# Memory attention placed in a recurrence's chunk loop, rope and weight sums beside seven-product pairs, and three more such pairs

## The chip, the cores and the metric

The kernel runs on one core of a Trainium2 chip. Its time is the device time of one execution in microseconds (us). Engines are named as the profile names them: PE multiplies matrices (PEld loads its weights), DVE, ACT and POOL work on vectors, SP issues most of the transfers (DMA). Each engine works through its own queue in order, and engines wait for one another by semaphores.

## The reference

One decoder layer on 1024 tokens of width 1024, in float32: a SwiGLU half-step (hidden width 2816), a mixer, another SwiGLU half-step, each with a norm ahead and behind. The mixer takes one projection `u @ w_in` and splits it for three branches, RWKV-7, windowed attention and cross-attention into 256 memory tokens, and 3 x 1024 gate columns:

```python
p_rwkv, p_swa, q_mem, gate_logits = _split(u @ w_in, IN_SIZES)
y_a = rwkv7_mix(p_rwkv, ...)                       # a recurrence over the tokens, 8 heads of 64
q_s, k_s = partial_rope(q_s, cos, sin), partial_rope(k_s, cos, sin)   # first 16 of 64 channels
y_b = sliding_window_gqa_sinks(q_s, k_s, v_s, swa_sinks)             # 8 query, 2 key heads, window 128
km, vm = jnp.split(mem_n @ w_kv, 2, axis=-1)
s = jnp.einsum('bshd,bmhd->bhsm', q_mem * 128 ** -0.5, km)           # 4 heads of 128
y_c = jnp.einsum('bhsm,bmhd->bshd', jax.nn.softmax(s, axis=-1), vm)
g_a, g_b, g_c = _split(jax.nn.sigmoid(gate_logits + gate_b), (D, D, D))
merged = g_a * (y_a @ w_branch[0]) + g_b * (y_b @ w_branch[1]) + g_c * (y_c @ w_branch[2])
h = h + rms_norm(merged @ w_out, mix_post_g)
```

## The kernel before

**Products.** A float32 product is made of three matmuls on values split in two: w_hi (ACT casts), w_lo (DVE subtracts), and the same for the moving side; L379 to L381 are the three. A strip is 128 output columns for 1024 tokens. A *plain* strip takes 8 blocks of the contraction x 2 halves of the tokens x 3 = 48 matmuls of 128x512. A *pair* of strips (`win_pair`) is done with seven products of 12 matmuls each (84 for two strips, 96 plainly), from sums of weights and of tokens: products collect in the PSUM tiles px, py and pz, ACT copies some to SBUF, and DVE adds them up (att<-px,part and so on) and so empties the banks.

**The order of the middle part.** First the pairs of `WIN_PAIRS`, nine of them, with gates 2 to 13 among them; beside pairs 4 to 7 a generator gives out small pieces of RWKV's triangular inverse between the products (`CORNER`). Then the RWKV chunk loop (`rwkv_chain`): 16 chunks of 64 tokens, each a chain of small matmuls (z, y, z, y, gram, z, and the transposes bkt) with DVE and ACT copies between. These take their PSUM banks in turn from one set of four (tag bg), so bkt waits until ACT has copied sv and uv out of y's bank. Behind each chunk's bkt stand six matmuls of gates 14 and 15, plain strips. POOL makes the weight sums (`ws`, L691) of three of the second SwiGLU's units beside the chunks, from loads issued on SP.

Then `rwkv_finish` (norm over the heads, and the output gate g_up: tiles ysq, var, yrs, gup), and `attention`: eight memory blocks of 128 tokens, then eight window blocks. A block has scores, soft (exponentials, shares), turn (transposes) and values. Between them PE is given *fill*: plain gate strips 16 to 23 and the branches' products, counted out by `FINISH` and `LUMPS`. The rope tables, k's rotation and each block's rotation of q run on DVE there, with the swapped channels loaded by small transfers. A branch's output goes to memory as y_d, and a scheduler places what is not kept in program order.

**Names.** msc: memory scores; mp, mst: exponentials, their maxima and sums; mptr, mpt: transposed shares in PSUM and SBUF; mpv, yo: values and output; km, vm, qm, kd: keys, values and queries.

Of the kernel before, what the change touches and what calls it, by code (L numbers as in the profile page):

```python
# [11 lines left out]
F32 = mybir.dt.float32  # L12
# [27 lines left out]
MAIN_PSUM = ("po", "px", "py", "pr", "pgate", "pq", "pb", "pw")  # L40
OPS = 8
KEEP = KP - OPS
LOOP_UNITS = 3
# [142 lines left out]
class MemoryBlock(Block):  # L186
    def soft(self, behind):
        pass

# [5 lines left out]
    def scores(self):  # L195
        V, S = self.nc.vector, self.nc.scalar
        scale = float(128 ** -0.5)
        banks = []
        st = self.pool.tile([P, 3, 4], F32, tag="mst", name="mst", bufs=2)
        for a in (0, 1):  # L200
# [3 lines left out]
            V.tensor_reduce(st[:, 0, 2 * a : 2 * a + 2], ps.rearrange("p (j k) -> p j k", k=MEM), AXX, ALU.max)  # L204
            banks.append(ps)
        V.tensor_scalar(st[:, 1], st[:, 0], -scale, None, ALU.mult)
        self.pr = self.pool.tile([P, 4, MEM], F32, tag="sc", name="mp", bufs=2)
        for i in range(4):
            S.activation(self.pr[:, i], banks[i // 2][:, (i % 2) * MEM : (i % 2 + 1) * MEM], ACT.Exp, scale=scale,
                         bias=st[:, 1, i : i + 1], accum_out=st[:, 2, i : i + 1])  # L210
        V.reciprocal(st[:, 0], st[:, 2])
        for i in range(4):
            V.tensor_scalar(self.pr[:, i], self.pr[:, i], st[:, 0, i : i + 1], 0.5, ALU.mult, ALU.mult)
        return last

    def turn(self):
        self.pt = self.pool.tile([P, 4, 2, P], F32, tag="pt", name="mpt", bufs=2)
        for a in (0, 1):
            ps = self.k.psum("mptr")
# [3 lines left out]
            self.copied = [self.nc.scalar.copy(self.pt[:, 2 * a : 2 * a + 2], ps.rearrange("p (j k c) -> p j k c", j=2, k=2))]  # L223
        return last

    def values(self):
        ps = self.k.psum("mpv")
        for h in range(4):
            for kt in (0, 1):
                self.mm(ps[:, h * P : (h + 1) * P], self.vm[:, kt, h * P : (h + 1) * P], self.pt[:, h, kt, :], start=kt == 0, stop=kt == 1)  # L230
        self.k.y_out(ps, self.y_d, self.b, self.pool)


class Builder:
# [364 lines left out]
    def ffn_in(self, f, x, form_d, first_d, parts, norm):  # L599

        nc, V = self.nc, self.nc.vector
        with self.tc.tile_pool(reuse_waits="tile", name="ffn_in", bufs=2) as pool:
# [13 lines left out]
            for j in range(KF):  # L616
                *pair, made = self.ffn_in_pair(f, j, pool, first_d)
                pairs.append(pair)
                skip = LOOP_UNITS if f == "ffn2" else 0
# [60 lines left out]
    def sums_in_loop(self, pool):  # L680

        beside, behind = {}, {}
        G = self.nc.gpsimd.tensor_tensor
# [1418 lines left out]
```

## Time and profile before

| what | number |
|---|---|
| median of 3 runs | 2245.7 us (2245.69 to 2249.21) |
| profiled execution, its span | 2246.46 us, 2244.6 us |
| PE, DVE, ACT, POOL busy | 2220.6, 1646.5, 1037.3, 96.7 us |
| chunk loop | about 1097 to 1204 us of the span |
| finish | about 1204 to 1234 us |
| memory blocks | 1234 to 1312 us |

A row of a timeline has start, length, engine, line, operation, output<-inputs, shape and count, and in brackets the idle time before it with what ended it. A row of windows has the stretch, its length, and for PE, PEld, DVE, ACT and POOL the busy time and the count; then the granted clock of PE as a share of full speed, the DMA share and GB/s. A row of waits has who waited for whom: total us, times, longest. Matmuls overlap, so the time of one is read from start to start.

### The profile page before, as it was taken

How to read it: one execution, taken by the hardware profiler on the slowest of the kernel's cores; microseconds unless marked ns; L12 is line 12 of the kernel's file. 1: busy time of each engine (PE TensorE's matmuls, PEld its weight loads, DVE VectorE, ACT ScalarE, POOL GpSimd, SP SyncE). 2: the span in 40 equal slices, each digit the busy share in tenths (PEclk: the TensorE clock that was granted, in tenths of full speed). 3: DMA queues.
4: the chain of work that ended last, by engine and by line, in shares of the span. 5: the costliest groups of instructions: out<-in, count | busy, mean ns of one | idle time of the engine just before them, and what ended most of it. 6: DMA issues, size and time to landing. Idle time of an engine off the chain costs nothing.

```text
span 2244.6 us, 34591 instructions
## 1 busy us (share of the span) xinstructions
PE 2220.6 (99%) x12280; PEld 1825.1 (81%) x12280; DVE 1646.5 (73%) x2769; ACT 1037.3 (46%) x1947; POOL 96.7 (4%) x166
## 2 busy tenths in 40 slices
PE   8999999999999999999999999999999999999998
PEld 6888888888887788888887887788888888887887
DVE  6988767766698887874467567794898887776576
ACT  6622333454555653444445564444663233345451
POOL 0000000000000011000253000000000000000000
PEclk9999999999999999999999999999999999999999
DMA  8565566686665446455574654464565555678663
GB/s 289 172 203 172 194 212 211 229 298 206 194 218 186 133 141 196 159 181 156 158 239 143 197 164 143 146 230 146 182 198 187 192 190 189 218 255 255 204 195 124
DMA packets 272236, 432.41 MB, mean 193 GB/s; under 512 B 50848, under 2 KB 89760, under 8 KB 271808
## 3 DMA queue, kind: packets, MB, share of 16 engines
q1 hardware_dynamic: 255392, 400.00, 55.1%
q10 hardware_dynamic: 15392, 29.17, 3.8%
q8 instruction: 96, 1.57, 0.3%
q0 software_dynamic: 1280, 1.05, 0.2%
q14 instruction: 76, 0.62, 0.1%
HBM read 292.75 MB, written 136.31 MB: 191 GB/s over the span
## 4 chain that ended last, share of the span: by engine, by line
PE 92%; DVE 4%; DMA 2%; issue 1%; ACT 1%; SPq 0%; DVEq 0%; ACTq 0%
PE px L379 9%; PE px L381 9%; PE px L380 9%; PE po L380 6%; PE po L381 6%; PE po L379 6%; PE pz L379 4%; PE pz L381 4%; PE pz L380 4%; PE pb L379 2%; PE pb L380 2%; PE pb L381 2%; PE pgate L379 2%; PE pgate L380 2%; PE pgate L381 2%; PE pr L379 2%
## 5 line engine op out<-in xcount | busy, mean ns | idle before, releaser
L302 ACT CAST w_hi<-w_raw 128x512 fp32r<-128x512 f32 x612 | 378.8, 620 | 696.9 <-PE px L380 191.7
L304 DVE TENSOR_TENSOR w_lo<-w_raw,w_hi 128x512 fp32r<-128x512 f32 x612 | 419.3, 687 | 182.3 <-ACT w_hi L302 164.7
L379 PE MATMUL po<-u,w_hi 128*128 128x512 f32 (+1 forms) x476 | 180.9, 380 | 0.0
L380 PE MATMUL po<-u,w_hi 128*128 128x512 f32 (+1 forms) x476 | 180.9, 380 | 0.0
L381 PE MATMUL po<-u,w_lo 128*128 128x512 f32 (+1 forms) x476 | 180.9, 380 | 0.0
L379 PE MATMUL px<-u,w_hi 128*128 128x512 f32 x388 | 151.2, 390 | 0.8 <-DVE km L1626 0.8
L379 PE MATMUL pz<-u,w_hi 128*128 128x512 f32 x388 | 151.2, 390 | 0.0
L381 PE MATMUL px<-u,w_lo 128*128 128x512 f32 x388 | 151.1, 389 | 0.0
L380 PE MATMUL px<-u,w_hi 128*128 128x512 f32 x388 | 150.9, 389 | 0.0
L380 PE MATMUL pz<-u,w_hi 128*128 128x512 f32 x388 | 150.9, 389 | 0.0
L381 PE MATMUL pz<-u,w_lo 128*128 128x512 f32 x388 | 150.9, 389 | 0.0
L379 PE MATMUL px<-f,w_hi 128*128 128x512 f32 x352 | 137.1, 390 | 0.3 <-DVE u L743 0.2
L380 PE MATMUL px<-f,w_hi 128*128 128x512 f32 x352 | 137.0, 389 | 0.0
L381 PE MATMUL px<-f,w_lo 128*128 128x512 f32 x352 | 136.9, 389 | 0.0
L488 DVE TENSOR_TENSOR u<-hid,u 128x512 fp32r<-128x512 f32 x114 | 78.4, 689 | 47.2 <-ACT u L487 46.5
L380 PEld LDWEIGHTS po<-u,w_hi 128*128 128x128 f32 x476 | 89.5, 188 | 17.2
L379 PEld LDWEIGHTS po<-u,w_hi 128*128 128x128 f32 x476 | 89.5, 188 | 17.0
L381 PEld LDWEIGHTS po<-u,w_lo 128*128 128x128 f32 x476 | 89.5, 188 | 16.8
L487 ACT CAST u<-hid 128x512 fp32r<-128x512 f32 x114 | 70.6, 620 | 66.0 <-DMA hid<-form_d 56.2
L379 PE MATMUL pr<-u,w_hi 128*128 128x512 f32 x224 | 87.6, 392 | 0.0
L380 PE MATMUL pr<-u,w_hi 128*128 128x512 f32 x224 | 87.3, 391 | 0.1
L381 PE MATMUL pr<-u,w_lo 128*128 128x512 f32 x224 | 87.2, 390 | 0.0
(451 smaller groups left out, 5213.9 us busy)
## 6 DMA issues: line engine op xcount, KB each, us to landing
w_raw<-in_ffn_in SPq DMA_DIRECT2D x224, 256.0 KB
hid<-form_d SPq DMA_DIRECT2D x154, 256.0 KB
w_raw<-in_win SPq DMA_DIRECT2D x112, 256.0 KB
form_d<-g SPq DMA_DIRECT2D x88, 256.0 KB
ws<-in_ffn_out SPq DMA_DIRECT2D x88, 256.0 KB
ffn_sum_d<-ws SPq DMA_DIRECT2D x88, 256.0 KB
w_raw<-ffn_sum_d SPq DMA_DIRECT2D x88, 256.0 KB
form_d<-h SPq DMA_DIRECT2D x66, 256.0 KB
```

Source lines behind the costliest of these rows:

```text
L302: self.nc.scalar.copy(hi, x)
L304: self.split_last = self.nc.vector.tensor_tensor(lo, x, hi.bitcast(F32), ALU.subtract)
L379: mm(out, wh, xh, start=first, stop=False, **kw)
L380: mm(out, wh, xl, start=False, stop=False, **kw)
L381: self.last_mm = mm(out, wl, xh, start=False, stop=last, **kw)
L487: self.nc.scalar.copy(hi, x)
L488: self.nc.vector.tensor_tensor(lo, x, hi.bitcast(F32), ALU.subtract)
```

## The change

1. **Three more pairs.** `GATES_FIRST` goes from 14 to 20: gates 14 to 19, plain before (two in the loop, four in the fill), become three pairs, twelve in all. `filling` starts with gate 21; gate 20 stays plain, most of it behind chunk 0.
2. **Memory attention in the loop.** Block i has its scores behind the odd chunk c = 2i + 1; the maxima and the exponentials in chunk c + 1, the shares there and in c + 2, the transposes behind chunk c + 2 and the values behind c + 3, with y_d stored from ACT's queue (`beside_chunks`). msc, mptr and mpv take banks of the other set of four (tag mm). The last blocks' remaining steps go into the finish (`between`). Gate 20's tanh and the table load for logarithm and exponential stand in chunk 1. `attention` has window blocks only, and the branches' order is 2, 0, 1.
3. **Rope and sums beside pairs 6 to 10.** `beside_pairs` gives out, between products: three units of weight sums (now on DVE), the rope tables, the rotation of k on DVE and of q on POOL in halves of 512 tokens, with loads on SP and stores to att_d on POOL. The inverse's pieces take pairs 4 and 5. Window blocks load rotated q and k.

The first place is PE's queue in the loop. Before, around one chunk's end:

```order
L1230 MATMUL y<-f,sv 64x64 x8
L1230 MATMUL z<-z,dinv 64x64 x8
L1230 MATMUL y<-center,f 64x64 x8
L1230 MATMUL gram<-f 128x128 x8
L1230 MATMUL z<-uv,bk 64x64 x8
L1270 MATMUL bkt<-ident,f 128x128 x4
L380 MATMUL pgate<-u,w_hi 128x512
L381 MATMUL pgate<-u,w_lo 128x512
L379 MATMUL pgate<-u,w_hi 128x512
```

Now, from an odd chunk's end to the next even chunk's:

```order
L1297 MATMUL bkt<-ident,f 128x128 x4
L105 MATMUL mptr<-ident,mp 128x128 x8
L102 MATMUL msc<-km_in,qm 128x256 x4
L1257 MATMUL z<-sv,gz 64x64 x8
L1257 MATMUL y<-gz,uv 64x64 x8
L1257 MATMUL y<-f,sv 64x64 x8
L1257 MATMUL z<-z,dinv 64x64 x8
L1257 MATMUL y<-center,f 64x64 x8
L1257 MATMUL gram<-f 128x128 x8
L1257 MATMUL z<-uv,bk 64x64 x8
L1297 MATMUL bkt<-ident,f 128x128 x4
L102 MATMUL mpv<-mpt,vm_in 128x128 x8
```

In the place of six gate matmuls stand a block's transposes and the next block's scores behind an odd chunk, and a block's values behind an even one.

The second place is ACT's queue in the same chunks. Before, one chunk and the end of the one ahead:

```order
L1250 COPY sv<-y 64x256 x2
L1250 COPY uv<-y 64x256 x2
L1271 COPY bk<-bkt 128x512
L1281 COPY y<-y 128x4x64
L1250 COPY sv<-y 64x256 x2
```

Now, the end of an odd chunk and the even one behind it:

```order
L1298 COPY bk<-bkt 128x512
L224 COPY mpt<-mptr 128x512 x2
L1308 COPY y<-y 128x4x64
L207 ACTIVATE mp,mst<-msc,mst 128x256 x4
L1277 COPY sv<-y 64x256 x2
L1277 COPY uv<-y 64x256 x2
L1298 COPY bk<-bkt 128x512
L1781 COPY yo<-mpv 128x512
```

The four exponentials stand behind the y copy and ahead of the copies of sv and uv; copies of mpt and yo come in between the chunks.

The third place is DVE's queue in a pair of strips (part and w_raw are sums and parts of weights, L1458 and L1490 the adds that empty px, py and pz). Before:

```order
L1458 TENSOR_TENSOR att<-pz,part 128x512
L304 TENSOR_TENSOR w_lo<-w_raw,w_hi 128x512
L329 TENSOR_TENSOR part<-w_raw 128x512
L304 TENSOR_TENSOR w_lo<-w_raw,w_hi 128x512 x2
L1458 TENSOR_TENSOR att<-py,part 128x512
L330 TENSOR_TENSOR w_raw<-w_raw 128x512
L331 TENSOR_TENSOR w_raw<-part,w_raw 128x512
L335 TENSOR_TENSOR w_raw<-w_raw 128x512
L304 TENSOR_TENSOR w_lo<-w_raw,w_hi 128x512
L304 TENSOR_TENSOR w_lo<-part,w_hi 128x512
L304 TENSOR_TENSOR w_lo<-w_raw,w_hi 128x512
L1458 TENSOR_TENSOR att<-px,part 128x512
```

Now, beside pair 6 or 7 (rope_x and rope_sw hold the weight blocks of a sum unit here; cos and sin are the tables in the making):

```order
L675 TENSOR_TENSOR rope_sw_9901<-rope_sw_9900,rope_sw_9901 128x512
L1675 TENSOR_SCALAR sin<-sin,rope_c 128x1024
L676 TENSOR_TENSOR rope_sw_9900<-rope_x_9898,rope_sw_9900 128x512
L1677 TENSOR_SCALAR cos<-sin 128x1024
L1490 TENSOR_TENSOR att<-px,part 128x512
L306 TENSOR_TENSOR w_lo<-w_raw,w_hi 128x512
L677 TENSOR_TENSOR rope_x_9898<-rope_sw_9901,rope_x_9898 128x512
L1678 TENSOR_SCALAR cos<-cos 128x1024
L1490 TENSOR_TENSOR att<-pz,part 128x512
L306 TENSOR_TENSOR w_lo<-w_raw,w_hi 128x512
L678 TENSOR_TENSOR rope_x_9899<-rope_x_9899,rope_x_9898 128x512
L1681 SCALAR_TENSOR_TENSOR sin<-cos,sin 128x1024 x2
```

Between the casts and the adds of the pair stand the sum's adds (L675 to L678) and the tables' steps on 128x1024.

The diff, cut to its core:

```diff
-MAIN_PSUM = ("po", "px", "py", "pr", "pgate", "pq", "pb", "pw")
+MAIN_PSUM = ("po", "px", "py", "pr", "pgate", "pq", "pb", "pw", "msc", "mptr", "mpv")
-LOOP_UNITS = 3
+PAIR_UNITS = 3
-BRANCHES = (0, 2, 1)
+BRANCHES = (2, 0, 1)
-CORNER = (4, 4)
-GATES_FIRST = 14
-GATES_EARLY = 16
-LUMPS = (24, 46)
-FINISH = (16, 6, 10)
+CORNER = (4, 4, 2)
+GATES_FIRST = 20
+LUMP = 46
+FINISH = (8, 6, 10)
...
-        src = self.att_d[2:6, :, cols].rearrange("j p t -> p j t")
-        nc.sync.dma_start(self.qs, src)
-        sw = self.sws[self.b % 2]
-        self.k.load_swapped(sw, src)
-        self.k.rotate(self.qs, sw, *(x[:, cols].rearrange("p t -> p () t").broadcast_to([P, 4, P]) for x in self.tables))
+        nc.sync.dma_start(self.qs, self.att_d[2:6, :, cols].rearrange("j p t -> p j t"))
...
+    def most(self, a):
+        ps = self.banks[a].rearrange("p (j k) -> p j k", k=MEM)
+        return self.nc.vector.tensor_reduce(self.st[:, 0, 2 * a : 2 * a + 2], ps, AXX, ALU.max)
+    def powers(self):
+        V, S, st = self.nc.vector, self.nc.scalar, self.st
+        scale = float(128 ** -0.5)
         V.tensor_scalar(st[:, 1], st[:, 0], -scale, None, ALU.mult)
-        self.pr = self.pool.tile([P, 4, MEM], F32, tag="sc", name="mp", bufs=2)
+        self.pr = self.pool.tile([P, 4, MEM], F32, tag="mp", name="mp", bufs=2)
         for i in range(4):
-            S.activation(self.pr[:, i], banks[i // 2][:, (i % 2) * MEM : (i % 2 + 1) * MEM], ACT.Exp, scale=scale,
+            S.activation(self.pr[:, i], self.banks[i // 2][:, (i % 2) * MEM : (i % 2 + 1) * MEM], ACT.Exp, scale=scale,
                          bias=st[:, 1, i : i + 1], accum_out=st[:, 2, i : i + 1])
-        V.reciprocal(st[:, 0], st[:, 2])
-        for i in range(4):
+    def shares(self, a):
+        V, st = self.nc.vector, self.st
+        if a == 0:
+            V.reciprocal(st[:, 0], st[:, 2])
+        for i in (2 * a, 2 * a + 1):
             V.tensor_scalar(self.pr[:, i], self.pr[:, i], st[:, 0, i : i + 1], 0.5, ALU.mult, ALU.mult)
-        return last
...
-        def unit(q, c):
-            a = a11, a12, a21, a22 = [pool.tile([P, KH, P], F32, tag="ws", name="ws", bufs=8) for _ in range(4)]
-            steps = ((a22, a21, a22, ALU.add), (a21, a11, a21, ALU.subtract), (a11, a22, a11, ALU.subtract), (a12, a12, a11, ALU.subtract))
-            for n, t in enumerate(a):
-                self.nc.sync.dma_start(t, self.io["ffn2_out"][n, q])
-            for n, x in enumerate(steps):
-                behind[c + 1 + n] = lambda x=x: G(*x)
...
+    def beside_pairs(self, pool, att_d):
+        nc, V, G = self.nc, self.nc.vector, self.nc.gpsimd
+        cos, sin = (pool.tile([P, T], F32, name=n, bufs=1) for n in ("cos", "sin"))
+        half = lambda n: [pool.tile([P, TH], F32, name=f"{n}{i}", bufs=1) for i in (0, 1)]
+        xs, sws = half("rope_x"), half("rope_sw")
+        blocks = [t.rearrange("p (k c) -> p k c", c=P) for t in xs + sws]
+        tables = self.rope_tables(cos, sin)
+        for q in range(PAIR_UNITS):
+            self.sums_loads("ffn2", q, blocks)
+            if q == 0:
+                next(tables)
+            yield
+            yield
+            self.sums_made("ffn2", q, blocks, self.split_last)
+            yield
+            if q < 2:
+                next(tables)
+            yield
+        for t in sws:
+            G.memset(t, 0.0)
+        rows = [(0, h) for h in (0, 1)] + [(j, h) for j in range(2, 6) for h in (0, 1)]
+        def load(i):
+            row, h = rows[i]
+            src = att_d[row][:, h * TH : (h + 1) * TH]
+            nc.sync.dma_start(xs[i % 2], src)
+            self.load_swapped(sws[i % 2], src)
+        load(0)
+        load(1)
+        yield
+        next(tables)
+        yield
+        for i, (row, h) in enumerate(rows):
+            cols = slice(h * TH, (h + 1) * TH)
+            self.rotate(V if row == 0 else G, xs[i % 2], sws[i % 2], cos[:, cols], sin[:, cols])
+            yield
+            nc.gpsimd.dma_start(att_d[row][:, cols], xs[i % 2])
+            if i + 2 < len(rows):
+                load(i + 2)
+            if row:
+                yield
...
                 q = 1 - q
                 mm(at(ps, p, q), n["gz"][:, q, p, 0, :], n["sv"][:, q, p, :])
             z = tile("z", [NPAIR, C])
-            V.tensor_copy(z, v3(ps))
+            copy = V.tensor_copy(z, v3(ps))
+            with self.tc.issue_after(copy.ins):
+                for f in copied.get(c, ()):
+                    f()
             sw = tile("sw", [NPAIR, C])
             for q in (0, 1):
-                scaled = G.tensor_tensor(sw[ROWS[q]], n["sv"][ROWS[q], q], wc[ROWS[q]].broadcast_to([64, NPAIR, C]), ALU.mult)
-            if c in behind:
-                with self.tc.issue_after(scaled.ins):
-                    behind[c]()
+                G.tensor_tensor(sw[ROWS[q]], n["sv"][ROWS[q], q], wc[ROWS[q]].broadcast_to([64, NPAIR, C]), ALU.mult)
             py = out(c - 1, before) if c else self.psum("y")
             for p, q in pairs:
                 self.solved = mm(at(ps, p, q, W4), n["d"][ROWS[q], p, :], z[ROWS[q], p, :])
             for q in (0, 1):
-                V.tensor_copy(n["uv"][ROWS[q], q], v3(ps, W4)[ROWS[q]])
+                self.kept = V.tensor_copy(n["uv"][ROWS[q], q], v3(ps, W4)[ROWS[q]])
             if not last:
                 values(nxt, py)
                 grams(nxt)
@@ -1328,10 +1355,12 @@
                     V.tensor_tensor(nxt["sv"][ROWS[q], q], t[ROWS[q]], sw[ROWS[q]], ALU.add)
                 masked(nxt, 1)
                 turned(nxt)
+            for f in slot.get(c, ()):
+                f()
             before, n = n, nxt
         return lambda: out(NC_ - 1, before)
-    def rwkv_finish(self, pool, early, y, bonus_d, ya_d):
+    def rwkv_finish(self, pool, early, y, bonus_d, ya_d, between):
         nc = self.nc
         V, S = nc.vector, nc.scalar
...
-        keep(S.preload_act_table_set("natural_log_exp_and_others"))
         square(0)
         square(1)
+        between.pop(0)()
         for h in (0, 1):
...
-            self.fill(FINISH[1], end)
+            if between:
+                between.pop(0)()
+            else:
+                self.fill(FINISH[1], end)
...
+    def logs(self):
+        self.tc.keep_in_program_order(self.nc.scalar.preload_act_table_set("natural_log_exp_and_others"))
+    def beside_chunks(self, i, block, copied, slot):
+        c = 2 * i + 1
+        late = c == NC_ - 1
+        add = lambda where, c, f: where.setdefault(c, []).append(f)
+        if i:
+            add(slot, c, self.before.turn)
+        def scores():
+            block.scores()
+            with self.tc.issue_after(self.kept.ins):
+                for a in (0, 1) if late else (0,):
+                    self.kept = block.most(a)
+                if late:
+                    block.powers()
+        add(slot, c, scores)
+        if not late:
+            add(copied, c + 1, lambda: block.most(1))
+            add(copied, c + 1, block.powers)
+            def shares():
+                with self.tc.issue_after(self.kept.ins):
+                    block.shares(0)
+            if c + 3 < NC_:
+                add(slot, c + 3, block.values)
+            add(slot, c + 1, shares)
+            add(copied, c + 2, lambda: block.shares(1))
+        self.before = block
...
+            small = lambda name: tc.tile_pool(reuse_waits="tile", name=name, bufs=2)
+            with chunks, small("chain_y") as y_pool, small("memory") as mem_pool:
+                y = y_pool.tile([P, NPAIR, T], F32, name="y", bufs=1)
+                blocks = [MemoryBlock(self, mem_pool, b, att_d=att_d, km=km, vm=vm, ahead=ahead, y_d=y_d[2]) for b in range(nb)]
+                beside, copied, slot = {0: [lambda: nc.sync.dma_start(km, km_d), blocks[0].load, blocks[1].load, lambda: nc.sync.dma_start(vm, vm_d)]}, {}, {}
+                for i, block in enumerate(blocks):
+                    if i > 1:
+                        beside[2 * i - 2] = [block.load]
+                    self.beside_chunks(i, block, copied, slot)
+                def gate():
+                    self.store = nc.scalar.dma_start
+                    self.gate_block(GATES_FIRST, u, gp, gate_d)
+                    self.store = nc.sync.dma_start
+                    self.logs()
+                slot[0] = [gate]
+                with small("chain") as pool:
+                    last = self.rwkv_chain(pool, early, fetched, pk_d, inv_d, y, beside, copied, slot)
+                    self.held = []
+                    self.fills, self.missing = self.filling(u, gp, gate_d, y_d), 0
+                    last()
...
+                def end():
+                    blocks[-1].values("bg")
+                    kd.extend(kv(f"kd{i}") for i in (0, 1))
+                    for i in (0, 1):
+                        for q in (0, 64):
+                            nc.sync.dma_start(kd[i][q : q + 64], att_d[0][i * 64 : i * 64 + 64])
+                def turn():
+                    for a in (0, 1):
+                        blocks[-1].shares(a)
+                    blocks[-1].turn("bg")
+                windows = [WindowBlock(self, None, b, att_d=att_d, ahead=ahead, kd=kd, y_d=y_d[1]) for b in range(nb)]
+                def first():
+                    blocks[-2].values("bg")
+                    for block in windows[:2]:
+                        block.load()
                 with tc.tile_pool(reuse_waits="tile", name="finish", bufs=3) as finish_pool:
-                    self.rwkv_finish(finish_pool, early, y, bonus_d, y_d[0])
+                    self.rwkv_finish(finish_pool, early, y, bonus_d, y_d[0], [first, turn, end])
...
-                self.attention(blocks, [42, 32] + [LUMPS[0]] * (nb - 2) + [LUMPS[1]] * nb, {0: [tables], 1: [keys], 2: [load_values], 4: [turn_values]})
+                self.attention(windows, turn_values)
```

More of the change, by code (lines that the diff above doesn't have):

```diff
@@ L186 @@
 class MemoryBlock(Block):
-    def soft(self, behind):
-        pass
     def load(self):
@@ L1684, in att_steps, with attention @@
             self.store(att_d[ATT_ROW[f], :, halves[0] * TH : halves[0] * TH + n], t)
-    def attention(self, blocks, lumps, others):
-        self.fill(lumps[0], blocks[0].scores())
-        for i, (block, n) in enumerate(zip(blocks, lumps)):
-            first = n * 2 // 3 if isinstance(block, MemoryBlock) else n // 2
+    def attention(self, blocks, turn_values):
+        self.fill(LUMP // 2, blocks[0].scores())
+        blocks[0].soft(())
+        for i, block in enumerate(blocks):
+            first = LUMP // 2
             if i + 1 < len(blocks):
@@ L1821, in mixer @@
             ahead = stay.enter_context(tc.tile_pool(reuse_waits="tile", name="ahead", bufs=1, side="right"))
-            km = ahead.tile([P, 4, MEM], F32, name="km_in")
-            vm = ahead.tile([P, 2, 512], F32, name="vm_in")
+            kv = lambda name: ahead.tile([P, T], F32, tag="kv", name=name, bufs=2)
+            km, vm = kv("km_in").rearrange("p (h m) -> p h m", m=MEM), kv("vm_in").rearrange("p (k c) -> p k c", c=512)
             nb = T // P
-            blocks = [MemoryBlock(self, None, b, att_d=att_d, km=km, vm=vm, ahead=ahead, y_d=y_d[2]) for b in range(nb)]
```

140 lines of the change are left out of this document (50 added, 90 removed).

## The prediction

> **What bounds the kernel now.** I read the page's head first, then the list of TensorE's waits, then the stretches that the change touches.
>
> ```profile
> span 2244.6 us, 34591 instructions
> PE 2220.6 (99%) x12280; PEld 1825.1 (81%) x12280; DVE 1646.5 (73%) x2769; ACT 1037.3 (46%) x1947; POOL 96.7 (4%) x166
> ```
> ```profile
> PE pq L1539 <- DMA mkv<-in_mkv_k: 6.4, 1, 6.4
> ...
> PE gup L1382 <- DVE yrs L1383: 0.5, 1, 0.5
> ```
>
> TensorE is busy 99% of the span, and the only wait of size is 6.4 us, long before the stretches of this change. So here a matmul that goes away is time that goes away, and a wait that comes in is time that comes in. The windows (PE, PEld, DVE, ACT, POOL busy; clock; DMA) show how much the other engines have left in two pairs of strips, the densest and a plain one.
>
> ```profile
> 943.00:962.00 19.00, 19.00 (x85) 15.74 (x84) 18.66 (x33) 6.29 (x11) 0.00 (x0) 1.00 0.32 110
> 1058.00:1077.00 19.00, 19.00 (x86) 15.73 (x85) 9.57 (x15) 9.06 (x15) 0.00 (x0) 1.00 0.32 111
> ```
>
> **Step 1, three more pairs.** Six gates as plain strips are 6 x 48 = 288 matmuls of 128x512; as three seven-product pairs they are 3 x 84 = 252. The pitch comes from eleven matmuls in a row, not from the printed length, since they overlap:
>
> ```profile
> 1083.70 0.39 PE L380 MATMUL px<-mix_form,w_hi 128*128 128x512 f32 x1
> ...
> 1085.97 0.39 PE L381 MATMUL pz<-mix_form,w_lo 128*128 128x512 f32 x1
> ```
>
> That row is the eleventh, so 2.27 us / 10 = 0.227 us each: -36 x 0.227 = **-8.2 us**. A pair lasts 84 x 0.227 = 19.1 us, and a plain one asks for 9.57 us of DVE and 9.06 of ACT (above), so its adds and casts stay behind the matmuls.
>
> **Step 2, memory attention in the chunk loop.** One chunk before, on PE, ACT and DVE:
>
> ```profile
> 1151.95 0.69 PE L1230 MATMUL z<-sv,gz 128*64 128x64 f32 x16
> ...
> 1156.56 0.66 PE L1270 MATMUL bkt<-ident,f 128*128 128x128 f32 x4
> 1156.97 0.48 PE L380 MATMUL pgate<-u,w_hi 128*128 128x512 f32 x1
> ...
> 1158.54 0.69 PE L1230 MATMUL z<-sv,gz 128*64 128x64 f32 x16
> ```
> ```profile
> 1153.76 0.37 ACT L1281 COPY y<-y 128x256 f32<-128x256 f32 x1 [2.46 <-PE y L1230]
> 1154.99 0.75 ACT L1250 COPY sv<-y 64x256 f32<-64x256 f32 x2 [0.86 <-PE y L1230]
> 1155.76 0.75 ACT L1250 COPY uv<-y 64x256 f32<-64x256 f32 x2
> ```
> ```profile
> 1157.45 0.86 DVE L1328 TENSOR_TENSOR sv<-ts,sw 64x256 f32<-64x256 f32 x2
> ```
>
> The period is 6.59 us: 5.02 of the chunk's own matmuls up to 1156.97, then 1.57 for six gate matmuls, of which 6 x 0.227 = 1.36 is work and 0.21 the change between kinds of matmul. DVE's chain ends with sv at 1158.31, 0.23 us before the next z: without any fill the period would still be 6.59. So fill under 1.57 us is free and missing fill saves nothing. What a memory block costs PE, from its place before:
>
> ```profile
> 1234.65 1.89 PE L103 MATMUL msc<-km_in,qm 128*128 128x256 f32 x8
> 1236.19 0.58 PE L379 MATMUL pgate<-u,w_hi 128*128 128x512 f32 x1
> 1236.60 0.40 PE L380 MATMUL pgate<-u,w_hi 128*128 128x512 f32 x1
> ```
>
> and a little later values and transposes, with the matmuls behind them:
>
> ```profile
> 1265.24 1.95 PE L103 MATMUL mpv<-mpt,vm_in 128*128 128x128 f32 x16
> 1267.02 1.04 PE L106 MATMUL mptr<-ident,mp 128*128 128x128 f32 x8
> 1267.82 0.48 PE L379 MATMUL pgate<-u,w_hi 128*128 128x512 f32 x1
> 1268.13 0.40 PE L380 MATMUL pgate<-u,w_hi 128*128 128x512 f32 x1
> ```
>
> From start to next start: scores 1.54, values 1.78, transposes 0.80, together 4.12; the first gate matmul behind each group has a pitch of 0.41 and 0.31, 0.18 and 0.08 too much, so 4.38 in all. The order puts 0.80 + 1.54 behind an odd chunk and 1.78 behind an even one, both over 1.57, so PE has enough to do there. What is new is on ACT: in even chunks four exps stand between the y copy and the sv and uv copies. Their length before, and what the bkt transposes wait for:
>
> ```profile
> 1272.21 0.48 ACT L209 ACTIVATE mp<-msc,mst 128x256 f32<-128x256 f32 x1 [3.42 <-DVE mst L206]
> ...
> 1274.02 0.63 ACT L302 CAST w_hi<-w_raw 128x512 fp32r<-128x512 f32 x1
> ```
> ```profile
> 1196.46 0.66 PE L1270 MATMUL bkt<-ident,f 128*128 128x128 f32 x4 [0.34 <-ACT uv L1250]
> ```
>
> Four exps take 1.81 us. Counted from z, the y copy ends at 2.18, so the exps end at 3.99 and the sv copies start there and not at 3.04 (1154.99): 0.95 later. The uv copies then end at 5.51, and bkt, which stood at 4.61, comes at 5.56. The mpv matmuls, the next z and the whole next chunk are queued behind bkt on PE, so the 0.95 is lost in each of the six even chunks 4 to 14: 5.7 us. Chunk 2 has neither fill nor memory matmuls: 1.57 idle. In chunk 1 the y copy stands behind two tanhs, a DMA issue and the table load that was in the finish before:
>
> ```profile
> 1205.31 1.28 ACT L1355 ACT_TABLE_LOAD   x1
> ```
>
> I put 0.7 us for it. Against these 8.0 us stand the changes of kind that go away: 15 x 0.21 = 3.2 in the loop and 8 x 0.26 = 2.1 in the blocks; about 1.0 comes back where memory groups meet the chunk's matmuls. **Loop: 8.0 - 3.2 - 2.1 + 1.0 = +3.7 us.** Bounds: -2.0 if the exps delay nothing (3.7 - 5.7), and +8 if the maxima of the scores, which stand ahead of the uv copies on DVE, cost their own 0.69 in six chunks as well.
>
> **Step 3, the finish.** Block 7 brings two maxima, their scaling, a reciprocal and four shares to DVE, the engine that the finish runs at.
>
> ```profile
> 1236.06 1.28 DVE L204 TENSOR_REDUCE mst<-msc 128x2 f32<-128x512 f32 x2
> ...
> 1240.55 1.14 DVE L213 TENSOR_SCALAR mp<-mp,mst 128x256 f32<-128x256 f32 x4
> ```
> ```profile
> 1204.80:1232.10 27.30, 26.20 (x111) 19.73 (x108) 24.52 (x31) 17.33 (x29) 9.78 (x7) 1.00 0.35 117
> ```
>
> That is about 2.8 us more on a DVE that is busy 24.5 of 27.3, less the 1.28 of the table load that left ACT's head and one cast of 0.69: **+1 us**. Below, -1: PE's whole idle time there is 1.1 us and could vanish; above, +4, if the second transposes' and values' copies on ACT come in the way too.
>
> **Step 4, the rest.** The tables and rotations leave the attention phase, where PE did not wait, so that gives nothing. The windows now start without memory blocks ahead, with their value transposes inside the first block: **+1 us** (0 to +3, two PSUM copies late).
>
> **Step 5, beside pairs 6 to 10.** Sums (12 adds of 128x512), tables and k's rotation go on DVE, q's rotation on POOL, 24 operations. The densest pair has 26 DVE operations: 15 of a plain pair took 9.57, so 23 take 14.7, and three of 128x1024 at 1.22 make it 18.4 of 19.1 us; the window 943:962 above had 18.66 of 19.00 and PE was busy all of it. The POOL part is another matter. In the finish POOL and DVE run such operations side by side:
>
> ```profile
> 1208.09 2.87 POOL L1350 TENSOR_TENSOR ysq<-y 128x512 f32<-128x512 f32 x2 [1.62 <-DVE ysq_lo L1352]
> ```
> ```profile
> 1208.53 1.53 DVE L304 TENSOR_TENSOR w_lo<-w_raw,w_hi 128x512 fp32r<-128x512 f32 x1
> ...
> 1221.14 0.68 DVE L304 TENSOR_TENSOR w_lo<-w_raw,w_hi 128x512 fp32r<-128x512 f32 x1
> ```
>
> The same DVE operation takes 1.53 beside POOL and 0.68 alone: 0.85 held. The 24 operations are spread over 16 slots of a product (12 matmuls, 2.73 us), 10.5 in a pair: DVE 9.57 + 10.5 x 0.85 = 18.5 of 19.1. I take **0**, with +8 as the upper end (rival B). SP's gate loads, queued behind the rotations' small loads, are asked for eight products (21.8 us) ahead.
>
> **Sum.** -8.2 + 3.7 + 1 + 1 + 0 = -2.5 us. The profiled execution took 2246.46 us (span 2244.6), 0.76 over the median of 2245.7, so 2243.96 on its own time is **2243.2 us** against the median.
>
> **Rivals.** *A, the exps delay nothing.* If bkt does not come later (its bank is freed by something else, or the mpv matmuls run ahead of it), the loop gives -2.0 and the sum is -8.2: 2237.5. For it: only one of sixteen bkt shows the wait, of 0.3. Against it: on ACT the copies cannot pass the exps.
> *B, POOL holds DVE up.* Place: the last pairs before the loop. If each rotation step holds DVE for its whole length, 1.3 us or more (2.87 for two above), a pair has 9.57 + 10.5 x 1.35 = 23.7 us of DVE in 19.1: 4.6 late per pair, 10.7 over 2.3 pairs; what is late is DVE's add that empties a product's bank, with 2.73 - 0.69 = 2.0 us to spare, and PE stands about 8 us: 2251. It decides from a mean hold of (19.1 - 9.57) / 10.5 = 0.9 us. For it: the measured 0.85 is just below. Against it: the rotation steps wait for their loads and are not packed that densely.
> [...]
> *C, the gain never comes:* the windows run out of fill, since six gates fewer are left to fill with. Each missing lump of 23 matmuls costs up to 5.2 us; two of them, 2253.
>
> **Numbers.** The forecast has 0.52, A 0.27, B 0.16, C 0.05. A measurement of this kernel tells 0.2%, 4.5 us, from no change: faster means under 2241.2, slower over 2250.2. Faster: nearly all of A and a fifth of the forecast, 0.36; slower: two thirds of B, half of C and 0.04 of the forecast, 0.17; within: 0.47. The forecast's own range is 2239 to 2248; with A's lower part and B's start, 2236 to 2250.5.
>
> **What would show it.** Step 1: 36 fewer matmuls of 128x512, each pair still 19.1 us. Step 2: even chunks of some 7.7 us with bkt 5.5 after z and a wait on ACT's uv, odd ones of 7.4 without; bkt at 4.6 in even chunks would be A. Step 5: no wait on DVE under px, py or pz before the loop; waits there of 2 us and more would be B. The forecast is wrong if a wait of over 3 us stands anywhere that this text does not name.

## The result: slower by 0.7%

The changed kernel takes 2262.8 us (median of 4 runs, 2259.9 to 2266.3) against 2246.3 us: a ratio of 1.0072, interval 1.0053 to 1.009. The forecast was 2243.2, its range 2236 to 2250.5. The profiled execution, 2259.9 us, is the fastest of the four, so what follows splits 13.6 of the median's 16.5 us. The head of its page:

```profile
span 2258.2 us, 34561 instructions
PE 2217.0 (98%) x12244; PEld 1822.4 (81%) x12244; DVE 1680.1 (74%) x2790; ACT 1051.1 (47%) x1967; POOL 118.7 (5%) x187
```

36 matmuls are gone (12280 to 12244), and the span is 13.6 us longer. Its list of TensorE's waits between 850 and 1400 us (total, times, longest) names where (sc are the scores of a window block, vt its transposed values):

```profile
PE bkt L1297 <- ACT uv L1277: 7.5, 7, 1.1
PE px L381 <- ACT part L1483: 6.1, 4, 2.5
PE sc L102 <- ACT vt L1962: 2.2, 1, 2.2
PE y L1257 <- ACT y L1308: 0.9, 1, 0.9
```

The windows by stage (length, then PE's busy time), of the kernel before: pairs, chunk loop, finish, attention.

```profile
895.20:1097.10 201.90, 201.90 (x1383) 164.93 (x1381) 127.29 (x217) 87.17 (x145) 8.43 (x15) 1.00 0.49 162
1097.10:1200.50 103.40, 102.86 (x1892) 86.00 (x1888) 65.04 (x161) 44.92 (x107) 50.54 (x73) 1.00 0.68 214
1200.50:1231.70 31.20, 30.10 (x157) 22.68 (x153) 25.87 (x35) 17.24 (x28) 9.78 (x7) 1.00 0.37 124
1231.70:1508.30 276.60, 276.60 (x1461) 226.92 (x1460) 200.87 (x426) 140.28 (x385) 2.45 (x3) 1.00 0.55 177
```

And of the changed kernel:

```profile
895.70:1164.70 269.00, 262.14 (x1636) 213.07 (x1634) 190.87 (x287) 119.33 (x193) 49.26 (x52) 0.99 0.58 193
1164.70:1292.90 128.20, 119.48 (x2042) 104.65 (x2040) 87.11 (x214) 66.30 (x178) 33.82 (x60) 1.00 0.47 140
1292.90:1324.30 31.40, 30.20 (x187) 24.53 (x182) 28.66 (x43) 20.53 (x42) 9.90 (x8) 1.00 0.64 187
1324.30:1523.80 199.50, 196.46 (x992) 155.35 (x991) 146.60 (x316) 97.81 (x274) 0.00 (x0) 0.99 0.57 185
```

With 0.227 us for a gate matmul and 1.54, 0.80 and 1.78 us for a block's scores, transposes and values, as in the prediction, each stage's change splits into work that was moved and time that was lost:

| stage | longer by | work moved | lost |
|---|---|---|---|
| pairs | 67.1 | 252 matmuls: 57.3 | +9.8 |
| chunk loop | 24.8 | -48 gate matmuls, 7 scores, 6 transposes, 6 values: 15.4 | +9.4 |
| finish | 0.2 | -27 gate matmuls, 2 transposes, 1 scores, 2 values: 0.6 | -0.4 |
| attention | -77.1 | -213 gate matmuls, 8 blocks: -81.4 | +4.3 |

The work sums to -8.1 us, where -8.2 was forecast; the loss to +23.1. The stages ahead (+0.5) and behind (-1.9), where nothing was changed, make up the rest to 13.6. So three questions: what is lost beside the pairs, in the loop, and at the start of the attention.

**The loop.** One even and one odd chunk on PE, and ACT in the even one:

```profile
1219.45 0.69 PE L1257 MATMUL z<-sv,gz 128*64 128x64 f32 x16
...
1225.16 0.65 PE L1297 MATMUL bkt<-ident,f 128*128 128x128 f32 x4 [1.09 <-ACT uv L1277]
1225.65 1.95 PE L102 MATMUL mpv<-mpt,vm_in 128*128 128x128 f32 x16
1227.53 0.69 PE L1257 MATMUL z<-sv,gz 128*64 128x64 f32 x16
...
1232.10 0.66 PE L1297 MATMUL bkt<-ident,f 128*128 128x128 f32 x4
1232.59 1.04 PE L105 MATMUL mptr<-ident,mp 128*128 128x128 f32 x8
1233.46 1.89 PE L102 MATMUL msc<-km_in,qm 128*128 128x256 f32 x8
1235.29 0.69 PE L1257 MATMUL z<-sv,gz 128*64 128x64 f32 x16
```
```profile
1221.26 0.37 ACT L1308 COPY y<-y 128x256 f32<-128x256 f32 x1 [2.74 <-PE y L1257]
1221.63 0.47 ACT L207 ACTIVATE mp<-msc,mst 128x256 f32<-128x256 f32 x1
...
1223.59 0.75 ACT L1277 COPY sv<-y 64x256 f32<-64x256 f32 x2
1224.36 0.74 ACT L1277 COPY uv<-y 64x256 f32<-64x256 f32 x2
```

The wait is the one forecast: the exponentials push the sv copies to 4.14 us after z and bkt to 5.71, with 1.09 us of waiting. The even chunk takes 8.08 us, the odd one 7.76; some 7.7 and 7.4 were forecast.

**The pairs.** Ahead of the first wait ACT loads tables four times, for sine, tanh, sine, tanh:

```profile
1073.01 1.28 ACT L1685 ACT_TABLE_LOAD   x1
...
1075.39 1.28 ACT L1493 ACT_TABLE_LOAD   x1
...
1077.93 1.28 ACT L1686 ACT_TABLE_LOAD   x1
...
1080.40 1.28 ACT L1493 ACT_TABLE_LOAD   x1
```

Later DVE's operations of 0.69 us take up to 3.53 us while POOL rotates q; and SP stands for the stores of rotated halves, with loads of gate weights queued behind, for which ACT waits in turn (SP's two longest waits and ACT's for gate weights, between 1060 and 1165 us):

```profile
1104.66 3.53 DVE L332 TENSOR_TENSOR w_raw<-w_raw 128x512 f32<-128x512 f32 x1
```
```profile
1105.08 1.30 POOL L1692 TENSOR_TENSOR rope_x<-rope_x,cos 128x512 f32<-128x512 f32 x1
1106.32 1.30 POOL L1693 TENSOR_TENSOR rope_sw<-rope_sw,sin 128x512 f32<-128x512 f32 x1
1107.70 1.64 POOL L1694 TENSOR_TENSOR rope_x<-rope_x,rope_sw 128x512 f32<-128x512 f32 x1
```
```profile
SPq L708 <- DMA att_d<-rope_x: 17.8, 7, 7.5
SPq L295 <- DVE w_lo L306: 16.1, 11, 5.1
...
ACT w_hi L304 <- DMA w_raw<-in_win: 7.5, 3, 4.1
```

DVE's operation ends at 1108.19, half a microsecond behind POOL's second step. Ahead of the longest wait both things stand one behind the other. A gate weight (w_raw) comes late, and the DVE operation that waited for it is then held:

```profile
1124.14 3.53 DVE L331 TENSOR_TENSOR part<-w_raw 128x512 f32<-128x512 f32 x1 [1.59 <-DMA w_raw<-in_win]
```

Four operations later DVE's L333 takes 1.71 us; ACT's cast waits for it, the copy part stands behind that cast, and px behind the copy:

```profile
1132.30 0.62 ACT L304 CAST w_hi<-w_raw 128x512 fp32r<-128x512 f32 x1 [0.96 <-DVE w_raw L333]
...
1133.34 0.58 ACT L1483 COPY part<-px 128x512 f32<-128x512 f32 x1
```
```profile
1131.05 0.39 PE L383 MATMUL pz<-mix_form,w_lo 128*128 128x512 f32 x1
1133.97 0.50 PE L381 MATMUL px<-mix_form,w_hi 128*128 128x512 f32 x1 [2.53 <-ACT part L1483]
1134.31 0.40 PE L382 MATMUL px<-mix_form,w_hi 128*128 128x512 f32 x1
```

How much of the loss each makes, the profile can't say: the queues wait for one another. It does show that a wait costs more than its idle time. From 1131.05 to 1134.31 there are two matmuls in 3.26 us: 2.53 of idle time, 2 x 0.227, and 0.27 more, since the last matmul ahead of the wait counts with its full 0.39 and the first behind it with 0.34. The five waits of this stage make 1.4 us of that.

### The profile page after: what moved, and what is told of

Its sections match the earlier page's. It is cut to its first block, busy times and chain, and to the rows that moved or that the text cites. A ratio compares the mean times of both kernels' runs of the same rounds, so it can differ in the third digit from the quotient of the medians.

```text
span 2258.2 us, 34561 instructions
## 1 busy us (share of the span) xinstructions
PE 2217.0 (98%) x12244; PEld 1822.4 (81%) x12244; DVE 1680.1 (74%) x2790; ACT 1051.1 (47%) x1967; POOL 118.7 (5%) x187
## 4 chain that ended last, share of the span: by engine, by line
PE 89%; DVE 5%; ACT 3%; DMA 2%; issue 1%; SPq 0%; ACTq 0%; DVEq 0%
PE px L381 9%; PE px L383 9%; PE px L382 9%; PE po L381 6%; PE po L383 6%; PE po L382 6%; PE pz L381 4%; PE pz L383 4%; PE pz L382 4%; PE pb L381 2%; PE pb L382 2%; PE pb L383 2%; PE pr L381 2%; PE pr L382 2%; PE pr L383 2%; PE pw L382 1%
## 5 line engine op out<-in xcount | busy, mean ns | idle before, releaser
L306 DVE TENSOR_TENSOR w_lo<-w_raw,w_hi 128x512 fp32r<-128x512 f32 x618 | 428.6, 695 | 189.8 <-ACT w_hi L304 177.0
L381 PE MATMUL pz<-u,w_hi 128*128 128x512 f32 x400 | 156.0, 390 | 0.7 <-ACT part L1483 0.7
L381 PE MATMUL px<-u,w_hi 128*128 128x512 f32 x400 | 155.8, 390 | 0.8 <-DVE km L1658 0.8
L383 PE MATMUL px<-u,w_lo 128*128 128x512 f32 x400 | 155.8, 389 | 0.0
L383 PE MATMUL pz<-u,w_lo 128*128 128x512 f32 x400 | 155.7, 389 | 0.0
L382 PE MATMUL pz<-u,w_hi 128*128 128x512 f32 x400 | 155.6, 389 | 0.0
L382 PE MATMUL px<-u,w_hi 128*128 128x512 f32 x400 | 155.6, 389 | 0.0
L381 PEld LDWEIGHTS px<-u,w_hi 128*128 128x128 f32 x400 | 75.1, 188 | 17.0 <-ACT r L489 1.6
L381 PEld LDWEIGHTS pz<-u,w_hi 128*128 128x128 f32 x400 | 75.2, 188 | 16.7 <-ACT part L1483 1.1
L383 PEld LDWEIGHTS pz<-u,w_lo 128*128 128x128 f32 x400 | 75.1, 188 | 15.7
```

Source lines behind the costliest of these rows:

```text
L306: self.split_last = self.nc.vector.tensor_tensor(lo, x, hi.bitcast(F32), ALU.subtract)
L381: mm(out, wh, xh, start=first, stop=False, **kw)
L382: mm(out, wh, xl, start=False, stop=False, **kw)
L383: self.last_mm = mm(out, wl, xh, start=False, stop=last, **kw)
```

## The experiments

All ratios are against runs of the kernel before on the same chip. The first four each undo one thing of the changed kernel.

**Q's rotation on DVE.**

```diff
-            self.rotate(V if row == 0 else G, xs[i % 2], ...)
+            self.rotate(V, xs[i % 2], ...)
```

> The rotation of q beside the pairs goes from POOL to DVE (24 operations of 128x512); loads, stores and everything else stay. If POOL's rotations hold DVE's operations (1.7 to 3.5 us in the changed kernel for what takes 0.69 alone), the waits of TensorE for ACT's part behind 1100 us (5.2 us) and the clock's half-speed stretch of 3.4 us behind them go: some 7 us less than the changed kernel, about 2256. If the gate weights come late because their loads stand behind the rotation's loads on SP, the waits stay and so does the time, about 2262. DVE has 24 x 0.6 = 14 us more work in 2.3 pairs, 16 of 19.1 us in a pair; if that is too much, waits of another kind come and the time is over 2263.

Measured: 2253.7 us, ratio 1.0036 (1.0024 to 1.0048), 9.1 us under the changed kernel. No DVE operation of 128x512 is over 1.0 us any more between 1090 us and the loop, and the half-speed stretch there is gone. TensorE's waits between 890 and 1165 us are down, but 2.2 of the 5.2 us behind 1100 remain, which were expected to go:

```profile
PE px L381 <- ACT part L1483: 4.0, 3, 1.7
```

The edit does not take the hold away alone. With the rotation on DVE, SP stands 11.8 us for the stores of the halves and not 17.8, 2.5 and not 7.5 at the longest. In the changed kernel ACT waited 7.5 us for gate weights, and DVE 1.9; here neither waits for one. SP's wait between 1060 and 1165 us:

```profile
SPq L708 <- DMA att_d<-rope_x: 11.8, 8, 2.5
```

**The exponentials behind the copies.** They are issued behind ACT's last copy of uv, everything else in its order.

```diff
                 values(nxt, py)
+                with self.tc.issue_after(self.last_uv.ins):
+                    for f in valued.get(c, ()):      # block.powers, before in copied
+                        f()
                 grams(nxt)
```

> In the even chunks the four exponentials stand behind ACT's copies of sv and uv and no longer ahead of them. If the place of the exponentials is what makes bkt late, all seven waits for uv (7.5 us) go, even chunks take 7.0 us and not 8.07 us, and the time is 6.5 us less than the changed kernel, about 2256. If the work is only pushed on, the copy of bk (now behind the exponentials) or the shares on DVE make the next chunk wait and the gain is under 2 us, over 2260.

Measured: 2258.2 us, ratio 1.0048 (1.0036 to 1.0061), 4.6 us under the changed kernel. The waits of bkt are gone but for 0.3 us (chunk 2's turns into one of 1.3 us for DVE's sv, and its period stays 6.51), and an even chunk takes 6.95 us from z to z:

```profile
PE bkt L1297 <- ACT uv L1277: 0.3, 1, 0.3
```
```profile
1221.30 0.69 PE L1257 MATMUL z<-sv,gz 128*64 128x64 f32 x16
...
1228.25 0.69 PE L1257 MATMUL z<-sv,gz 128*64 128x64 f32 x16
```

The loop is 6.3 us shorter in its profile (121.9 against 128.2); that is the first case of the expectation. The gain in time is smaller. The profiled execution, 2258.3, had a wait of 3.1 us with a half-speed stretch beside the pairs, in a part that the edit leaves alone.

**The sines together.**

```diff
-        nc.scalar.activation(ang, ang, ACT.Sin)
-        nc.scalar.activation(n, n, ACT.Sin, scale=-1.0, bias=self.half_pi)
+        with self.tc.high_priority(offset=self.urgent):
+            nc.scalar.activation(ang, ang, ACT.Sin)
+            nc.scalar.activation(n, n, ACT.Sin, scale=-1.0, bias=self.half_pi)
```

> The two sine evaluations of the rope tables stand next to one another on ACT, so that two table loads of 1.28 us replace four beside the gates' tanh. If the first wait beside the pairs (1.7 us at 1085 us) comes from ACT being late by four table loads, it shrinks to under 0.5 us: 1 to 2 us less, about 2261. If holding ACT for 4.8 us in one piece is as bad, no change, 2262 to 2264.

Measured: 2257.9 us, ratio 1.0049 (1.0036 to 1.0061). The wait at 1085 us is gone, so ACT's table loads made it. The gain of 4.9 us is more than that wait of 1.7; between the two profiled executions it is 2.0, and the stage of the pairs is 2.8 us shorter. The later waits of px fell too (from 4.4 us in three to 2.9 in two), while one of pz rose from 0.7 to 1.1. That the queues came to the rotation less late is my reading; the run doesn't show it by itself.

**No rotation of q.** The windows use q without rope.

```diff
-        rows = [(0, h) for h in (0, 1)] + [(j, h) for j in range(2, 6) for h in (0, 1)]
+        rows = [(0, h) for h in (0, 1)]
```

> The rotation of q is left out altogether (the windows use q without rope): 24 POOL operations, their 8 stores and their 40 loads on SP are gone; k's rotation, tables and sums stay. This is the whole price of the rotation beside the pairs, by either reason: the waits behind 1100 us and the half-speed stretch go, 7 to 8 us less than the changed kernel, about 2255. If it is no less than the run with q on DVE, SP's loads cost nothing; if it is 3 us less or more, they have a price of their own. If the stretch is slow for another reason (three denser pairs as such), about 2262.

Measured: 2252.8 us, ratio 1.0029 (1.002 to 1.0037): 10.0 us under the changed kernel, and 0.9 under q on DVE, which the spread of the runs (2249.4 to 2256.3) doesn't tell apart. By the expectation, SP's loads would cost nothing. That doesn't follow, since q on DVE had already shortened SP's standing, and the run with a third pair of buffers, below, speaks against it.

**Three edits together**: q on DVE, the exponentials behind, the sines together.

> The three edits together: q rotated on DVE, the exponentials behind ACT's copies of sv and uv, the two sines next to one another. If the three causes are separate, the gains add: from 2253.7 (q on DVE alone) down by the 4.6 to 6.5 of the exponentials and the 1 to 1.7 of the first wait beside the pairs, 2246 to 2248, no different from the kernel before. If they share one cause (each only lets queues catch up that are late anyway), the sum is well short: over 2250.

Measured: 2247.8 us, ratio 1.0004 (0.9995 to 1.0014): level with the kernel before. It is within the 2246 to 2248 of separate causes. But the single edits gained 18.6 us together and these 15.0, so they overlap by 3.6.

**Five edits**: these, and ACT's copies of vt early, and the table load of chunk 1 behind its copies.

```diff
+                        with tc.high_priority(offset=self.urgent):
                             nc.scalar.copy(vt[:, a * 4 : a * 4 + 4], ...)
...
-                    self.logs()                       # in gate(), behind chunk 0
+                valued[1] = [self.logs]
```

> The three edits, and the copies of the transposed window values (vt) early on ACT, and the table load of chunk 1 behind that chunk's copies of sv and uv. If the wait of sc for vt (1.9 to 2.5 us) brings the half-speed stretch of the clock of 3.4 to 6.8 us behind it, both go, and chunk 1 loses its 0.9 us wait: some 4.5 us less than the three edits, 2242 to 2244, faster than the kernel before by about the 8.2 us of the 36 matmuls less what the loop still loses. If the stretch has nothing to do with that wait, it stays at about 1360 us and the time is 2245 to 2246.

Measured: 2242.2 us, ratio 0.9981 (0.9972 to 0.999): faster than the kernel before. The waits of sc for vt and of y for ACT are gone, chunk 1 takes 6.90 us and not 7.98, and the attention stage, up to the first matmul of pw, takes 195.0 us, not 199.5 (199.3 with the three edits). With the wait for vt the half-speed stretch behind it is gone too. TensorE's list from 890 us on begins

```profile
PE px L381 <- ACT part L1486: 3.1, 2, 2.0
```

**The order of scores and transposes**, with q on DVE:

```diff
-        if i:
-            add(slot, c, self.before.turn)
         add(slot, c, scores)
+        if i:
+            add(slot, c, self.before.turn)
```

> Q on DVE, and in odd chunks the next block's scores ahead of the block's transposes, so that z follows the transposes and not the scores. The start-to-start time from scores to z is 1.83 us in the loop and was 1.54 us to a gate matmul before. If z is late because it follows the scores, odd chunks get 0.2 to 0.3 us shorter in seven chunks: 1.5 to 2 us less than q on DVE alone, about 2252. If it is the price of any change of kind on TensorE, odd chunks stay at 7.76 us and the time at 2253.7.

Measured: 2254.2 us, ratio 1.0034 (1.0022 to 1.0047): no change from q on DVE alone. An odd chunk of it:

```profile
1229.32 1.89 PE L102 MATMUL msc<-km_in,qm 128*128 128x256 f32 x8
1231.05 1.04 PE L105 MATMUL mptr<-ident,mp 128*128 128x128 f32 x8
1232.01 0.69 PE L1257 MATMUL z<-sv,gz 128*64 128x64 f32 x16
```

Scores 1.73 and transposes 0.96, together 2.69; in the other order 0.87 and 1.83, together 2.70. So it is not what z follows. The loss goes with the changes of kind; what makes it is not shown.

**A third pair of buffers**, with the five edits: a half's loads are asked for three halves ahead, not two.

```diff
-        half = lambda n: [... for i in (0, 1)]
+        half = lambda n: [... for i in range(3)]
...
-            if i + 2 < len(rows):
-                load(i + 2)
+            if i + 3 < len(rows):
+                load(i + 3)
```

> The five edits, and a third pair of buffers for the rotation's halves, so that a half's loads are asked for one half earlier. What is left of the waits beside the pairs with q on DVE (3.1 us in two waits, behind DVE standing 2.8 us for a rotation load) goes if it is the loads' round through SP and the store of two halves before: about 3 us less than the five edits, 2239. If DVE's work as such is too much there, the waits stay: 2242.

Measured: 2242.3 us, ratio 0.9981 (0.9972 to 0.9989). The px wait falls from 3.1 to 1.7 us in the profiles, but the time does not move: about 2239 was expected and not found. In the five edits no gate weight was late by more than 0.4 us any more, so there was little left for earlier loads to mend.

**The third pair of buffers alone**, on the changed kernel, q on POOL:

> The changed kernel with that third pair of buffers alone; q's rotation stays on POOL. If the loads behind waits on SP are what costs, the waits beside the pairs go as they do with q on DVE: 2254. If it is POOL holding DVE's operations, they stay, DVE still shows operations of 1.7 to 3.5 us, and the time is 2260 to 2263.

Measured: 2253.6 us, ratio 1.0033 (1.0021 to 1.0045): as much as q on DVE gave. DVE is still held, for 1.1 to 3.5 us in 16 operations, and yet the waits are down, the 1.7 us of the table loads among what is left:

```profile
1105.34 3.54 DVE L337 TENSOR_TENSOR w_raw<-w_raw 128x512 f32<-128x512 f32 x1
```
```profile
PE px L381 <- ACT part L1483: 3.0, 2, 1.7
```

So the theory that POOL's hold alone makes the waits falls: the holds sum to 16.5 us against 17.7, and SP's standing for the stores is down to 9.9 us. DVE no longer waits for a gate weight; ACT still does, for 5.9 us in two waits, and the second of them, 4.3 us, ends just ahead of the PE wait of 1.3 that is left. Late loads alone were not tested, because q on DVE took away both. In the profiles the stage of the pairs, 269.0 us in the changed kernel, takes 263.2 here, 263.9 with q on DVE and 262.7 without q's rotation, where the work moved into it alone would make 259.2. So 5.1 to 6.3 of the 9.8 us lost there hang on the rotation; the rest of the 9 us between the medians lies elsewhere or in the spread of the runs.

**The five edits without q's rotation.**

> The five edits with q's rotation left out altogether (the windows use q without rope): the floor under the rotation beside the pairs. If q on DVE costs 3.1 us of waits in the five edits, this is 2239; if it costs nothing that the run can tell, 2242.

Measured: 2238.0 us, ratio 0.9965 (0.9952 to 0.9977). That is 4.2 us under the five edits, so q's rotation beside the pairs still costs that on DVE, and it is 8.0 us under the kernel before, about what the 36 matmuls weigh. (By the ratios, 0.9965 against 0.9981, it is 3.6 us.)

**POOL again, with buffers and the other four edits.**

> Q's rotation stays on POOL, with the third pair of buffers; the exponentials behind the copies, the sines together, vt early, chunk 1's table load later. The one edit of the five that is undone is q on DVE, and the buffers are new. If early loads alone take POOL's holds off the path once the other queues are in time, the waits beside the pairs are under 1.5 us and the time is 2240 to 2242, as with q on DVE. If the holds still cost, there are waits of 3 us and more and the time is 2244 or more.

Measured: 2244.5 us, ratio 0.9991 (0.9982 to 0.9999), over the 2240 to 2242 of the first theory and 2.3 us over the five edits. The largest single wait beside the pairs is 0.9 us, and one of the two names is now DVE's add itself:

```profile
PE px L381 <- DVE att L1493: 1.6, 3, 0.9
...
PE px L381 <- ACT part L1486: 1.2, 2, 0.8
```

The five waits sum to 2.8 us, between the two cases of the expectation, and the one of 0.9 us, at 1076, ends ahead of POOL's first step. Against the right neighbour, q on DVE with the same buffers, it is 2.2 us more and 3.0 in the profiled stage of the pairs, but the intervals of the two ratios overlap. That the holds keep a price of about 2 us when the loads are earlier is likely, and not shown.

## Why the prediction was wrong

**The failing step is step 5**, the rotation and sums beside the pairs at 0 us, with 9.8 lost in its stage: 6.9 us of PE idle, 1.7 at half clock and 1.4 around the five waits. Its place and engine were named by rival B (2251, chance 0.16), and of B the price was near, which is in part luck: B took 32 us of holds, there were 17.7, and the third pair of buffers shows that holds of that size are not enough.

Two terms were wrong. First, the hold was judged by its mean, 0.85 us a step from one row of the finish, against 0.9 that would decide for B. The mean came out no worse, 17.7 us over 24 steps or 0.74; but it came in pieces of up to 2.8 us, more than the 2.0 that the prediction itself gave an add to empty a bank, since the three steps of a half run back to back and DVE's three longest operations ended 0.56 or 0.57 us behind the second. The reason given against B, that the steps are not packed densely, was wrong within a half. Second, the sentence on SP ("asked for eight products ahead") costed the loads at nothing. SP issued no gate load between 1098.3 and 1115.1 us: it stood 7.3 us for steps and stores of the rotation, and 5.1 for a DVE operation to free a buffer. DVE and ACT waited 9.4 us for gate weights; earlier loads alone, with the holds as they were, brought 9 us. And the four table loads between sine and tanh were in the order of the changed kernel, but nowhere in the sum: 1.7 us of waiting in the profile, taken away by putting the sines together.

**Step 2** was right in its mechanism: the exponentials delay bkt in the even chunks (5.56 us after z forecast, 5.71 measured; 5.7 us in all forecast, 6.5 measured in the same six chunks, 7.5 with chunk 2's), and moving them takes it away. Chunk 1's wait was 0.9 for 0.7, and chunk 2's period 6.51 for 6.59. Rival A falls with that. Too small was one term, the 1.0 us that "comes back where memory groups meet the chunk's matmuls". From the rows, an odd chunk spends 0.49 + 0.87 + 1.83 from bkt to z, against 0.41 + 0.80 + 1.54 assumed: 0.44 more in six chunks; chunk 1, without transposes, 0.37 and an even chunk 0.18 more: 4.1 us together. The loop lost 9.4, and 5.8 of the forecast fell to it (8.0 - 3.2 + 1.0).

**Step 3**, the finish at +1 (-1 to +4): -0.4 measured. Right within its bounds.

**Step 4**, the start of the windows at +1 (0 to +3): the two late copies of vt were the right place, with a wait of 2.2 us, and the half-speed stretch of the clock behind it, 1.7 us, was not in the sum. The attention lost 4.3 in place of -1.1 (this +1 less the 2.1 of the blocks' changes of kind). Taking vt early shortens the stage by 4.5; it is then 0.2 us under what the moved work alone would make, with 0.7 of idle time in it, so of the 2.1 about 0.9 came.

**Step 1** stands: 36 matmuls fewer, -8.1 us of work. In the kernel without q's rotation, and with most waits mended, the time comes out lower by as much, though other gains and losses are in it.

What stays open: how the rotation's price divides between holds and late loads, since no run has late loads without POOL's holds; why the sines together gained more than their wait; and what makes the changes of kind dearer in the loop.

## What to carry to other kernels

Count work that moves into a stage where one engine is full by its place in each queue, not by its share of busy time, nor by a mean. Here POOL's steps held DVE's operations for 17.7 us, SP stood 17.8 us for the stores of the rotated halves, and ACT and DVE waited 9.4 us for the gate weights queued behind. Giving those loads one more buffer was as good here (2253.6 us) as moving the work (2253.7). Where a chain waits for a copy, put the new work behind that copy and not ahead; this edit of the order alone gave 4.6 us here. Count the table loads that a function brings when it comes between others of another table: here there were four of 1.28 us, and the edit that puts the sines together gained 4.9 us.

## What the hardware showed

**Half a clock behind a wait.** The windows of the changed kernel around its two longest waits in this part:

```profile
1131.50:1135.00 3.50, 1.03 (x4) 0.86 (x5) 3.45 (x4) 2.63 (x5) 3.18 (x4) 0.99 0.25 90
1134.90:1138.40 3.50, 3.50 (x10) 2.73 (x9) 2.00 (x2) 0.14 (x2) 2.84 (x4) 0.51 0.57 183
1349.90:1353.40 3.50, 1.32 (x10) 1.12 (x8) 2.39 (x10) 3.50 (x13) 0.00 (x0) 1.00 0.54 180
1353.40:1356.90 3.50, 3.50 (x9) 2.43 (x8) 3.46 (x8) 1.52 (x4) 0.00 (x0) 0.52 0.64 226
```

A wait of 2.53 and one of 2.18 us are each followed by 3.4 us at a granted clock of about 0.5 (0.51 and 0.52 in the windows). In the first stretch the matmuls start 0.43 us apart and not 0.227; from 1134.77 to 1138.42 there are eight in 3.65 us, 1.8 us more than at full pace. Half of 3.4 us makes my estimate of 1.7 us on top of each such wait. Over the thirteen profiles, 13 of the 15 single waits of 1.83 us and more between 760 and 1600 us had such a stretch (of 3.4 or 6.8 us) behind them, and none of those up to 1.79 us. The two without were 2.73 us, with the third pair of buffers alone, and 1.97 us, in the five edits; what sets them apart no run shows. That the stretch follows a wait is shown, and that it went in the five edits, when the wait of 2.18 us for vt was taken away; the wait alone was not tested. At 782 us, in a part that is the same in all kernels, it stands behind waits of 1.90 us (five edits with the third pair) and 1.86 (five edits without q's rotation), and not behind those of 1.23 in the kernel before and the changed one; so it adds to the spread of the runs, by my estimate from these profiles.

**A hold over more than one instruction.** In the changed kernel DVE operations of 0.69 us took up to 1.78 us beside one step of POOL's rotation and 3.49 to 3.53 beside two in a row, 14 of them over 1.0 us and 17.7 us over their own length together; with the same steps on DVE, none beside the pairs. The three longest began 0.42 to 0.44 us ahead of the first of POOL's two steps (1104.66 against 1105.08 for the one of 3.53 shown above) and ended 0.56 or 0.57 us behind the second: having begun first did not spare them.
